# Sliding-window stores: 237 direct stores of 32 rows become 60 row scatters of 128 rows

## The chip, the cores and the metric

One core of one Trainium2 chip. The metric is the device time of one execution in microseconds (us), median of several runs. The profile is one further execution; its span is some 2 us shorter than the run time. All runs quoted are fast: granted clock 1.0. A kernel is compared with runs of the kernel before on the same chip.

## The reference

```python
batch, c, h, w = (16, 64, 64, 64); window_size = 8; stride = 4      # float32
n_h = n_w = 15
result = np.zeros((batch, n_h, n_w, c, 8, 8))
for i in range(n_h):
    for j in range(n_w):
        result[:, i, j] = x[:, :, 4*i : 4*i + 8, 4*j : 4*j + 8]
```

Nothing is computed. 16.78 MB are read, 58.98 MB written (each pixel lies in up to four windows).

## The kernel before

The whole input lies in SBUF as `L`, one partition per (image b, channel half ch, band q of 16 image rows), partition p = 8b + 4ch + q. For each window column j and slot s, DVE packs one window per partition into a tile `g` of 8 KB per partition, 1 MiB in all. Partition (b, ch, q) then holds half a row of the output, window row i = 4q + s. The last slot needs rows from the next band and has no window for q = 3.

```python
    HQ = 4; CH = 2; CL = 32; RB = 16; NSLOT = 4
    L = lpool.tile([P, CL, RB, W], f32)                       # 128 KB per partition
    o_v = out.rearrange("b i j (ch cl) r w -> i j b ch (cl r w)", ch=CH)
    ...                                                       # 16 loads of 1 MiB on ACT
    for j in range(NW):
        for s in range(NSLOT):
            g = gpool.tile([P, CL, WS, WS], f32, name="g")    # 9 buffers
            chunks = NCH if j == 0 and s == 0 else 1          # first tile in four pieces
            ...
                if s < NSLOT - 1:
                    nc.vector.tensor_copy(out=g[:, cs], in_=L[:, cs, s*ST : s*ST + WS, cols])
                else: ...                                     # copy of half a window, shuffle of the other
                for q in range(HQ):
                    i = NSLOT * q + s
                    if i < NH:
                        nc.sync.dma_start(out=o_v[i, j, :, :, ...], in_=g[q::HQ, cs, :, :])
```

One store takes every fourth partition: 32 rows of 8 KB, 256 KB. On the HBM side its shape is 16 images x 2 channel halves x 2048 elements.

Of the kernel before, what the change touches and what calls it, by code (L numbers as in the profile page):

```python
# [1 line left out]

# [4 lines left out]


@with_exitstack  # L10
def kernel(
    ctx: ExitStack,
    tc: tile.TileContext,
    x: bass.AP,
    window_size: int,
    stride: int,
    out: bass.AP,
):
    nc = tc.nc
    P = nc.NUM_PARTITIONS  # L20

    B, C, H, W = x.shape
    Bo, NH, NW, Co, WSo, WSo2 = out.shape
    WS = int(window_size)
    ST = int(stride)
    assert Bo == B and Co == C and WSo == WS and WSo2 == WS

    f32 = mybir.dt.float32

    HQ = 4  # L30
    CH = P // (B * HQ)
    CL = C // CH
    RB = H // HQ
    NSLOT = RB // ST
    assert WS == 2 * ST

    lpool = ctx.enter_context(tc.tile_pool(name="lpool", bufs=1))
    gpool = ctx.enter_context(tc.tile_pool(name="gpool", bufs=9))


    L = lpool.tile([P, CL, RB, W], f32)
    x_v = x.rearrange("b (ch cl) (hq r) w -> hq (b ch) cl (r w)", ch=CH, hq=HQ)
    o_v = out.rearrange("b i j (ch cl) r w -> i j b ch (cl r w)", ch=CH)
    NCH = 4
    cw = CL // NCH
    for k in range(NCH):
        for q in range(HQ):
            nc.scalar.dma_start(  # L48
                out=L[q::HQ, k * cw : (k + 1) * cw, :, :],
                in_=x_v[q, :, k * cw : (k + 1) * cw, :],  # L50
            )

    nxt = [min(p + 1, 31) for p in range(32)]
    CFREE = CL * WS * WS
    for j in range(NW):
        cols = slice(j * ST, j * ST + WS)
        for s in range(NSLOT):
            g = gpool.tile([P, CL, WS, WS], f32, name="g")
            chunks = NCH if j == 0 and s == 0 else 1
            n = CL // chunks  # L60
            for k in range(chunks):
                cs = slice(k * n, (k + 1) * n)
                if s < NSLOT - 1:
                    nc.vector.tensor_copy(out=g[:, cs, :, :], in_=L[:, cs, s * ST : s * ST + WS, cols])  # L64
                else:

                    nc.vector.tensor_copy(out=g[:, cs, 0:ST, :], in_=L[:, cs, s * ST : RB, cols])  # L67
                    nc.vector.stream_shuffle(out=g[:, cs, ST:WS, :], in_=L[:, cs, 0:ST, cols], mask=nxt)  # L68
                for q in range(HQ):
                    i = NSLOT * q + s  # L70
                    if i < NH:
                        nc.sync.dma_start(  # L72
                            out=o_v[i, j, :, :, k * CFREE // chunks : (k + 1) * CFREE // chunks],
                            in_=g[q::HQ, cs, :, :],
                        )


# [1 line left out]
_INS = ['x', 'window_size', 'stride']  # L79
_OUTS = [((16, 15, 15, 64, 8, 8), 'float32')]  # L80

_NUMBERS = {'window_size': 8, 'stride': 4}


# [26 lines left out]
```

## Time and profile before

| | value |
|---|---|
| time | 222.07 us (221.17 to 224.38, 3 runs) |
| loads | to 45.8 us, 409 GB/s |
| stores | 50 to 220 us, 339 to 345 GB/s, DMA share 0.95 to 0.97 |
| 8 KB store packet | median 309 ns, mean 365 ns |
| DVE busy | 82.9 us, 37% |

Packet times are from the trace's record of each DMA packet: when it started on its DMA engine and how long it took. The page and the windows are read in the prediction.

### The profile page before, as it was taken

Reading aid. Unit: us, or ns where it says so; the run is one execution under the profiler, and the core shown is the slowest. Engines: PE = TensorE matmul, PEld = TensorE weight load, DVE = VectorE, ACT = ScalarE, POOL = GpSimd, SP = SyncE. Lnnn points to the kernel's source line nnn. Section 1 sums busy time; section 2 is a strip of 40 time slices with the busy share of each in tenths; the row PEclk is TensorE's granted clock in tenths of the full one; section 3 lists DMA queues with packets and bytes.
Section 4 is the critical chain, followed back from the end, with each engine's and each line's share of the span. In section 5 each row is a group of like instructions: output and inputs, shape, how many; then the busy total and the mean of one; then the engine's idle time right before and its main releaser. Section 6 shows DMA issues by size and latency. Waiting matters only on the chain.

```text
span 222.1 us, 564 instructions
## 1 busy us (share of the span) xinstructions
DVE 82.9 (37%) x93; POOL 0.2 (0%) x4
## 2 busy tenths in 40 slices
DVE  0000000069946354454526453535454545430000
POOL 0000000000000000000000000000000000000000
DMA  5999999928999999999999999999999999999995
GB/s 210 418 409 412 412 413 409 412 103 285 337 356 351 328 350 344 334 344 337 341 339 348 359 341 342 353 347 335 360 353 342 332 354 334 329 347 335 326 359 215
DMA packets 15733, 75.81 MB, mean 341 GB/s; under 512 B 4049, under 2 KB 4049, under 8 KB 8657
## 3 DMA queue, kind: packets, MB, share of 16 engines
q1 hardware_dynamic: 11376, 59.00, 74.9%
q10 hardware_dynamic: 4352, 16.78, 18.9%
q14 instruction: 5, 0.03, 0.0%
HBM read 16.78 MB, written 58.98 MB: 341 GB/s over the span
## 4 chain that ended last, share of the span: by engine, by line
SPq 59%; DMA 22%; issue 5%; DVE 2%; ACTq 1%; DVEq 0%
SPq L72 59%; DMA L<-in_x_dram 20%; DMA out_dram<-g 3%; ACTq L48 1%; DVE g L64 1%; DVE g L68 1%; DVE g L67 0%; DVEq L64 0%; DVEq L67 0%
## 5 line engine op out<-in xcount | busy, mean ns | idle before, releaser
L64 DVE COPY g<-L 128x2048 f32<-128x2048 f32 (+1 forms) x48 | 55.1, 1159 | 93.2 <-DMA out_dram<-g 47.9
L68 DVE STREAM_SHUFFLE g<-L 128x1024 f32<-128x1024 f32 x15 | 19.2, 1278 | 0.0
L67 DVE COPY g<-L 128x1024 f32<-128x1024 f32 x15 | 10.4, 693 | 21.9 <-DMA out_dram<-g 21.9
L68 DVE LOAD_MASK_SELECT g<-L x15 | 0.2, 15 | 0.0
L92 POOL MEMSET const-bfloat16-1.0<- 128x1 bf16 x1 | 0.1, 102 | 0.0
L92 POOL MEMSET const-uint8-127<- 128x1 uint8 x1 | 0.1, 102 | 0.0
L92 POOL MEMSET const-float32-0.0<- 128x1 f32 x1 | 0.1, 99 | 0.2 <-issue 0.2
L92 POOL MEMSET const-float32-1.0<- 128x1 f32 x1 | 0.1, 99 | 0.0
## 6 DMA issues: line engine op xcount, KB each, us to landing
out_dram<-g SPq DMA_DIRECT2D x221, 256.0 KB, 3.8
L<-in_x_dram ACTq DMA_DIRECT2D x16, 1024.0 KB, 10.8
out_dram<-g SPq DMA_DIRECT2D x16, 64.0 KB, 5.1
```

What stands on the lines that cost most here:

```text
L48: nc.scalar.dma_start(out=L[q::HQ, k * cw : (k + 1) * cw, :, :], in_=x_v[q, :, k * cw : (k + 1) * cw, :],)
L64: nc.vector.tensor_copy(out=g[:, cs, :, :], in_=L[:, cs, s * ST : s * ST + WS, cols])
L67: nc.vector.tensor_copy(out=g[:, cs, 0:ST, :], in_=L[:, cs, s * ST : RB, cols])
L68: nc.vector.stream_shuffle(out=g[:, cs, ST:WS, :], in_=L[:, cs, 0:ST, cols], mask=nxt)
L72: nc.sync.dma_start(out=o_v[i, j, :, :, k * CFREE // chunks : (k + 1) * CFREE // chunks], in_=g[q::HQ, cs, :, :],)
L92: nc = _bacc.Bacc("TRN2", target_bir_lowering=False, num_devices=1)
```

## The change

The intent: one scatter per tile instead of four direct stores. Each partition has an index, computed once: the output row (of 8 KB) that it fills. A scatter takes all 128 partitions; the tile's j and s are an offset added to the index. Where a row is to be skipped (q = 3 in the last slot), a second index is past the end and the row is dropped. The scatters are issued from gpsimd (POOL), so the stores leave SP; loads are dealt to SP and ACT; the first tile is no longer cut in four.

```diff
-            nc.scalar.dma_start(                                  # loads
+            (nc.sync, nc.scalar)[q % 2].dma_start(
...
+    nc.gpsimd.iota(pi[:, :], pattern=[[0, 1]], base=0, channel_multiplier=1)
+    ...                     # nine DVE instructions on 128x1: idx = b*450 + q*120 + ch
+    ...                     # idx_last = idx, plus 14400 where q == 3
+    o_v = out.rearrange("b i j (ch cl) r w -> (b i j ch) (cl r w)", ch=CH)
...
-                for q in range(HQ):
-                    i = NSLOT * q + s
-                    if i < NH:
-                        nc.sync.dma_start(out=o_v[i, j, ...], in_=g[q::HQ, cs, :, :])
+            st = nc.gpsimd.indirect_dma_start(
+                out=o_v,
+                out_offset=bass.IndirectOffsetOnAxis(ap=(idx_last if last else idx)[:, 0:1], axis=0),
+                in_=g.rearrange("p c r w -> p (c r w)"), in_offset=None,
+                element_offset=(s * NW + j) * CH * CFREE,
+                bounds_check=B * NWIN * CH - 1, oob_is_err=False)
+            tc.declare_no_dep(st.ins, group="stores", reason="each store writes rows of its own")
```

More of the change, by code (lines that the diff above doesn't have):

```diff
@@ L28 @@
     f32 = mybir.dt.float32
+    i32 = mybir.dt.int32
+    ALU = mybir.AluOpType
     HQ = 4
@@ L34 @@
     NSLOT = RB // ST
-    assert WS == 2 * ST
+    NWIN = NH * NW
+    CFREE = CL * WS * WS
+    assert HQ == 4 and CH == 2 and WS == 2 * ST
     lpool = ctx.enter_context(tc.tile_pool(name="lpool", bufs=1))
+    ipool = ctx.enter_context(tc.tile_pool(name="ipool", bufs=1))
     gpool = ctx.enter_context(tc.tile_pool(name="gpool", bufs=9))
@@ L42 @@
     x_v = x.rearrange("b (ch cl) (hq r) w -> hq (b ch) cl (r w)", ch=CH, hq=HQ)
-    o_v = out.rearrange("b i j (ch cl) r w -> i j b ch (cl r w)", ch=CH)
     NCH = 4
@@ L51, with itile @@
             )
+    def itile(name):
+        return ipool.tile([P, 1], i32, name=name)
+    pi, tb, tq, tc_, idx, idx_last = (itile(n) for n in ("pi", "tb", "tq", "tc", "idx", "idx_last"))
+    nc.gpsimd.iota(pi[:, :], pattern=[[0, 1]], base=0, channel_multiplier=1)
+    nc.vector.tensor_scalar(out=tb[:, :], in0=pi[:, :], scalar1=3, scalar2=None, op0=ALU.logical_shift_right)
+    nc.vector.tensor_scalar(out=tc_[:, :], in0=pi[:, :], scalar1=2, scalar2=1, op0=ALU.logical_shift_right, op1=ALU.bitwise_and)
+    nc.vector.tensor_scalar(out=tq[:, :], in0=pi[:, :], scalar1=HQ - 1, scalar2=None, op0=ALU.bitwise_and)
+    nc.vector.tensor_scalar(out=tb[:, :], in0=tb[:, :], scalar1=float(NWIN * CH), scalar2=None, op0=ALU.mult)
+    nc.vector.tensor_tensor(out=tb[:, :], in0=tb[:, :], in1=tc_[:, :], op=ALU.add)
+    nc.vector.tensor_scalar(out=tc_[:, :], in0=tq[:, :], scalar1=float(NSLOT * NW * CH), scalar2=None, op0=ALU.mult)
+    nc.vector.tensor_tensor(out=idx[:, :], in0=tb[:, :], in1=tc_[:, :], op=ALU.add)
+    nc.vector.tensor_scalar(out=tq[:, :], in0=tq[:, :], scalar1=float(HQ - 1), scalar2=float(2 * B * NWIN * CH), op0=ALU.is_equal, op1=ALU.mult)
+    nc.vector.tensor_tensor(out=idx_last[:, :], in0=idx[:, :], in1=tq[:, :], op=ALU.add)
+    o_v = out.rearrange("b i j (ch cl) r w -> (b i j ch) (cl r w)", ch=CH)
     nxt = [min(p + 1, 31) for p in range(32)]
-    CFREE = CL * WS * WS
     for j in range(NW):
@@ L58 @@
             g = gpool.tile([P, CL, WS, WS], f32, name="g")
-            chunks = NCH if j == 0 and s == 0 else 1
-            n = CL // chunks
-            for k in range(chunks):
-                cs = slice(k * n, (k + 1) * n)
-                if s < NSLOT - 1:
-                    nc.vector.tensor_copy(out=g[:, cs, :, :], in_=L[:, cs, s * ST : s * ST + WS, cols])
-                else:
-                    nc.vector.tensor_copy(out=g[:, cs, 0:ST, :], in_=L[:, cs, s * ST : RB, cols])
-                    nc.vector.stream_shuffle(out=g[:, cs, ST:WS, :], in_=L[:, cs, 0:ST, cols], mask=nxt)
-                for q in range(HQ):
-                    i = NSLOT * q + s
-                    if i < NH:
-                        nc.sync.dma_start(
-                            out=o_v[i, j, :, :, k * CFREE // chunks : (k + 1) * CFREE // chunks],
-                            in_=g[q::HQ, cs, :, :],
-                        )
+            last = s == NSLOT - 1
+            if not last:
+                nc.vector.tensor_copy(out=g[:, :, :, :], in_=L[:, :, s * ST : s * ST + WS, cols])
+            else:
+                nc.vector.tensor_copy(out=g[:, :, 0:ST, :], in_=L[:, :, s * ST : RB, cols])
+                nc.vector.stream_shuffle(out=g[:, :, ST:WS, :], in_=L[:, :, 0:ST, cols], mask=nxt)
+            st = nc.gpsimd.indirect_dma_start(
+                out=o_v,
+                out_offset=bass.IndirectOffsetOnAxis(ap=(idx_last if last else idx)[:, 0:1], axis=0),
+                in_=g.rearrange("p c r w -> p (c r w)"),
+                in_offset=None,
+                element_offset=(s * NW + j) * CH * CFREE,
+                bounds_check=B * NWIN * CH - 1,
+                oob_is_err=False,
+            )
+            tc.declare_no_dep(st.ins, group="stores", reason="each store writes rows of its own")
+            tc.add_to_no_dep_group("stores", st.ins)
 _INS = ['x', 'window_size', 'stride']
```

## The prediction

> **What bounds the kernel now.** The kernel is pure data movement: 16.78 MB of images are loaded, the vector engine (DVE) packs windows into tiles g of 1 MiB, 58.98 MB of windows are stored. I read the busy strip first, to find the stages.
>
> ```profile
> ## 2 busy tenths in 40 slices
> DVE  0000000069946354454526453535454545430000
> ...
> DMA  5999999928999999999999999999999999999995
> GB/s 210 418 409 412 412 413 409 412 103 285 337 356 351 328 350 344 334 344 337 341 339 348 359 341 342 353 347 335 360 353 342 332 354 334 329 347 335 326 359 215
> ```
>
> Each slice is 5.55 us. Three stages: loads at about 410 GB/s up to 45 us, a hole near 46 to 51 us (slice 9, 103 GB/s), then stores at about 343 GB/s. So the stores run 16% slower than the loads on the same 16 DMA engines, although those are called busy throughout. A table by stage confirms it; its columns are window, length, DVE busy, POOL busy, clock, DMA share, GB/s:
>
> ```profile
> 14.00:45.50 31.50, 1.19 (x3) 0.00 (x0) 1.00 1.02 409
> 45.50:51.00 5.50, 4.58 (x7) 0.00 (x0) 1.00 0.29 73
> 51.00:100.00 49.00, 29.31 (x32) 0.00 (x0) 1.00 0.96 339
> 100.00:150.00 50.00, 23.85 (x26) 0.00 (x0) 1.00 0.96 345
> ...
> 200.00:220.00 20.00, 0.00 (x0) 0.00 (x0) 1.00 0.95 339
> ```
>
> From 200 us on DVE has nothing left to do and the rate is still 339 GB/s: neither DVE nor the nine g buffers set it. It is either the transfers or the sync engine (SP) that issues them. The chain that ended last names SP:
>
> ```profile
> SPq 59%; DMA 22%; issue 5%; DVE 2%; ACTq 1%; DVEq 0%
> ```
>
> The timeline and the view of the store's line show how SP issues:
>
> ```profile
> 99.71 25.75 SPq L72 DMA_DIRECT2D out_dram<-g  x34
> ```
>
> ```profile
> L72 SPq DMA_DIRECT2D out_dram<-g x237: 536/644/1385, 14.4 to 217.3; - x119
> ...
> DMA to landing us min/median/max: 1.9/3.8/5.2
> ```
>
> SP issues without a break, 34 stores in 25.75 us, 0.757 us each; a tile needs four of them (one per row group q), 3.03 us. The next line has the shortest, median and longest issue in ns: 0.54 us where nothing holds it up, 0.64 usually. A 256 KB store is two 8 KB packets on each of 16 DMA engines. The packet records of the trace give an 8 KB packet at 309 ns for 60% of them (2 x 309 = 0.62 us), but 364 ns on average. So an issue takes about as long as the transfer that it starts, and each can make the other wait. Where I follow one DMA engine from packet to packet, about a quarter of the stores start after a small hole, and their first packet is then often over 500 ns; at the very first store after the hole all 16 first packets took 539 to 700 ns and the 16 after them 309. Loads, with 16 packets per engine and issue, have 159 ns (median) per 4 KB packet and 164 on average. My reading: **the stores lose their 16% because they are fed in small pieces, just in time**. 309 ns per packet would be 16 x 8192 B / 309 ns = 424 GB/s.
>
> [...]
>
> **The change part by part.**
> - *Removed*: 237 store issues on SP. *Added*: 60 scatters on POOL, one per tile, of 128 rows of 8 KB (96 rows in the 15 tiles with s = 3, where the rows q = 3 lie past the end and are skipped). The rows stay 45 x 128 + 15 x 96 = 7200, the bytes the same 58.98 MB in the same 8 KB packets. Per DMA engine that is 450 packets if the rows spread evenly, 8 per scatter, with one completion instead of four per tile.
> - *Loads* now from two queues, SP and ACT. The loads already run at 409 to 418 GB/s with issues of 0.61 us for 1 MiB (one landing each 2.7 us): worth about 0.
> - *Index arithmetic*: one iota and nine DVE instructions on 128x1, long over before the first load chunk lands (DVE first works at 13.9 us). Worth 0.
> - *The first tile is no longer cut in four*: 3 x 256 KB that were stored under the loads move behind them. The DMA engines were full in both places: loads end 0.79 MB / 410 GB/s = 1.9 us earlier, and the bytes are paid later. But the hole grows: before, a 0.43 us copy and a 0.54 us issue came ahead of the first late store; now a full 1.23 us copy and the first descriptor generation.
> - *Order*: the scatters are declared independent; each waits only for its copy and, from the ninth on, for the scatter eight earlier. Some eight scatters of about 2.5 us can be queued, so POOL's delay is hidden as long as its throughput is enough.
>
> The sum. Last load lands 46.2 - 1.9 = 44.3 us, DVE starts 44.5, copy done 45.7. First scatter's descriptors and first packet: 2 us, an estimate (the shortest issue to landing before was 1.9 us; nothing shows a scatter). Stores begin at 47.7. Rate: packets of 309 ns with what remains of disturbance. In runs of packets that follow each other without a hole I found about 330 and 347 ns for the first and second of a store; fewer completions should help, so I take 330 ns (an estimate): 450 x 0.330 = 148.5 us, 397 GB/s. Tail from the last packet to the end, as before: 219.9 to 222.1, 2.2 us. Together 47.7 + 148.5 + 2.2 = 198.4; I say **199 us**, 10% faster.
>
> **The rivals.**
> 1. *POOL becomes the bound.* A tile on the DMA engines is 148.5 / 60 = 2.5 us. DVE's copies per tile are (45 x 1.226 + 15 x 0.693) / 60 = 1.09 us[...]. If generation takes G and the two exclude each other wholly, POOL needs 1.09 + G. Up to G = 1.4 us nothing is lost; G = 1.8 gives 2.9 per tile, 174 us, 224 in all, no gain; G = 2.3 gives 253.[...] Against it: the author's choice of this form, and the eight scatters of slack, which smooth but do not add throughput.
> 2. *HBM writes are the limit, not the feeding.* Then 343 GB/s stays: 172 us of stores, 222 in all, same. For it: even unbroken runs show a third of second packets over 330 ns. Against it: 60% of packets at exactly 309 ns[...].
> 3. *Full gain*: every packet at 309 ns, 139 us, 189 in all.
> 4. *Uneven engines*: skipped rows falling on the same DMA engines[...]. If a few engines get all 8 rows in every scatter they carry 480 packets instead of 450: 10 us more, 209.
>
> **Range and chances.** Central 199. Rivals 3 and 4 span 189 to 209; rival 1 has the long tail upward, rival 2 sits at 222. I give POOL as bound about 0.25 (half of it beyond 226 us), HBM as limit about 0.12. Low 187, high 228; faster 0.70, same 0.13, slower 0.17.
>
> **What would show it.** Right: stores at 385 to 420 GB/s in the strip, DMA share 1.0, mean 8 KB packet 320 to 340 ns, DVE waiting for landed stores, POOL's issues waiting for scatters to complete. POOL as bound: DMA share well under 0.9 in the store stage, scatters issued back to back, the chain on POOL's queue, and gaps that line up with DVE copies. HBM as limit: share 1.0, 343 GB/s, packets still 364 ns on average. Start wrong: first store later than 48 us. The prediction is wrong if G, which no trace here shows, exceeds about 1.5 us[...].

Passages that say of the hardware what no trace or run of this case shows are cut out of the recorded texts, here and in the expectations; the cuts are marked. "The two exclude each other wholly" in rival 1 was an assumption; e4 measures what there is of it. "Descriptors" and "generation" (G) name the time that POOL is busy with one scatter, 0.96 to 2.43 us in the changed kernel; what POOL does in that time no trace shows.

## The result, and the profile after

201.17 us (200.99 to 201.24, 4 runs) against 222.22 us: faster, ratio 0.904 (95% interval 0.8973 to 0.9108). A ratio is the mean time of one kernel's fast runs over that of the other's fast runs of the same rounds, so it is not quite the ratio of the medians.

The busy strip of the changed kernel, in 40 slices of 4.98 us:

```profile
DVE  2000000009996646464657474746464646430000
POOL 0000000006888787545455555555555555540000
DMA  5999999972999999999999999999999999999961
GB/s 189 419 405 410 410 414 410 409 303 92 401 398 410 406 405 400 408 405 413 405 411 415 408 405 411 411 406 405 413 406 408 406 413 406 406 411 414 419 286 43
```

After the hole the stores now run at the rate of the loads; only the last two slices fall off. The same by stage (window, length, DVE busy, POOL busy, clock, DMA share, GB/s):

```profile
14.00:43.00 29.00, 0.00 (x0) 0.00 (x0) 1.00 1.03 410
...
100.00:150.00 50.00, 28.57 (x31) 26.98 (x21) 1.00 1.01 408
...
180.00:190.00 10.00, 0.00 (x0) 0.00 (x0) 1.00 1.01 415
190.00:194.00 4.00, 0.00 (x0) 0.00 (x0) 1.00 0.64 268
194.00:196.00 2.00, 0.00 (x0) 0.00 (x0) 1.00 0.34 139
```

The store rate went from 343 to 408 GB/s at a DMA share of 1.01 instead of 0.96. Loads are as fast as before, two queues or one. The packet records give the same picture: the mean 8 KB packet fell from 365 to 322 ns. At the end half of the DMA engines have their last packet at about 191.2 us and the other half at about 195.4 us, so the last 4 us run at half rate or less. POOL, new in this kernel, is seen best in the groups (count, busy us, mean ns, idle before and its cause):

```profile
L86 POOL DMA_INDIRECT out_dram<-g,idx x45 | 60.5, 1344 | 86.4 <-DVE g L82 45.2
...
L86 POOL DMA_INDIRECT out_dram<-g,idx_last x15 | 19.6, 1308 | 11.4 <-DVE g L85 9.6
```

In the timeline around the start, two scatters show what stretches them:

```profile
44.62 3.50 DVE L82 COPY g<-L 128x2048 f32<-128x2048 f32 x3 [42.46 <-DMA L<-in_x_dram]
46.14 2.10 POOL L86 DMA_INDIRECT out_dram<-g,idx  x1 [45.19 <-DVE g L82]
...
53.84 1.26 DVE L85 STREAM_SHUFFLE g<-L 128x1024 f32<-128x1024 f32 x1
54.45 0.96 POOL L86 DMA_INDIRECT out_dram<-g,idx  x1 [0.30 <-issue]
```

Beside a run of copies the first scatter took 2.10 us; beside a shuffle one took 0.96 us. The median is 1.38. Even so, POOL is busy only half of the store stage, and it is 4% of the chain that ended last ("issue" is time for which the profile shows no wait):

```profile
DMA 51%; issue 34%; POOL 4%; POOLq 1%; PEldq 0%
```

A scatter's issue to landing is 18.7 us: some eight are queued.

One more thing is in the packet counts. The scatters' queue has 8640 packets: 7200 rows, 60 x 16 = 960 completions, and 480 more of 4 bytes, exactly the 15 x 32 skipped rows. I infer that a skipped row still costs a tiny packet; the 4-byte packets take 7 to 9 ns each, so it costs almost nothing here. (The page's HBM line counts 62.91 MB written, 3.93 MB too many, which is 480 rows of 8 KB: it seems to count skipped rows in full. The queue moved 58.99 MB.)

### The profile page after: what moved, and what is told of

Same layout as the page of the kernel before. It is cut to its first block, busy times and chain, and to the rows that moved or that the text cites. A ratio compares the mean times of both kernels' runs of the same rounds, so it can differ in the third digit from the quotient of the medians.

```text
span 199.2 us, 395 instructions
## 1 busy us (share of the span) xinstructions
DVE 83.8 (42%) x99; POOL 80.4 (40%) x65
## 3 DMA queue, kind: packets, MB, share of 16 engines
q0 software_dynamic: 8640, 58.99, 73.2%
HBM read 16.78 MB, written 62.91 MB: 400 GB/s over the span
## 4 chain that ended last, share of the span: by engine, by line
DMA 51%; issue 34%; POOL 4%; POOLq 1%; PEldq 0%
DMA out_dram<-g,idx_last 51%; POOL out_dram L86 4%; POOLq L127 1%; POOLq L86 0%; POOL pi L62 0%; PEldq L127 0%
## 5 line engine op out<-in xcount | busy, mean ns | idle before, releaser
L86 POOL DMA_INDIRECT out_dram<-g,idx x45 | 60.5, 1344 | 86.4 <-DVE g L82 45.2
L82 DVE COPY g<-L 128x2048 f32<-128x2048 f32 x45 | 55.1, 1235 | 75.3 <-DMA L<-in_x_dram 42.5
L86 POOL DMA_INDIRECT out_dram<-g,idx_last x15 | 19.6, 1308 | 11.4 <-DVE g L85 9.6
## 6 DMA issues: line engine op xcount, KB each, us to landing
out_dram<-g,idx POOLq DMA_INDIRECT x45, 18.7
```

Source lines behind the costliest of these rows:

```text
L82: nc.vector.tensor_copy(out=g[:, :, :, :], in_=L[:, :, s * ST : s * ST + WS, cols])
L86: st = nc.gpsimd.indirect_dma_start(out=o_v, out_offset=bass.IndirectOffsetOnAxis(ap=(idx_last if last else idx)[:, 0:1], axis=0), in_=g.r ...
```

## The experiments

The time agreed with the prediction at once. The question was whether its reason did: that 256 KB stores, issued just in time by one queue, starved the DMA engines.

| run | time, us | ratio to before | store stage, GB/s | mean packet, ns | over 330 ns |
|---|---|---|---|---|---|
| before | 222 to 224 | 1 | 339 to 345 | 362 | 36% |
| changed kernel | 201.17 | 0.904 | 406 to 409 | 323 | 17% |
| e1_two_queues | 218.75 | 0.985 | 346 to 354 | 366 | 32% |
| e4_copies_on_act | 201.94 | 0.908 | 406 to 409 | 323 | 16% |
| e6_chunked_start | 200.61 | 0.902 | 401 to 409 | 323 | 17% |
| e9_half_scatters | 237.51 | 1.068 | 306 to 315 | (4 KB packets) | |
| e5_wide_direct (wrong rows) | 194.78 | 0.875 | 415 to 421 | 314 | 11% |
| e10_four_buffers (wrong rows) | 194.71 | 0.871 | 416 to 420 | 314 | 11% |
| e7_deep_direct (wrong rows) | 195.80 | 0.880 | 409 to 420 | 315 | 3% |
| e11_two_rows (wrong rows) | 196.05 | 0.877 | 406 to 417 | 315 | 10% |
| e12_one_row (wrong rows) | 199.15 | 0.891 | 399 to 409 | 315 | 0.2% |
| e14_one_row_by_image (wrong rows) | 226.05 | 1.010 | 327 to 352 | 364 | 36% |
| e13_direct_and_scatter | 291.34 | 1.300 | 251 to 325 | 385 | 35% |
| e15_start_filled | 203.32 | 0.909 | 408 to 409 | 323 | 16% |

Store rates are from windows between 50 and 180 us (e15 from 100 on); packet figures are 8 KB packets that start between 60 and 180 us, from the trace's records. "Wrong rows" means that the kernel writes all output bytes, but to other rows than it should.

### e1: the kernel before with two issuing queues

```diff
-                        nc.sync.dma_start(
+                        (nc.sync, nc.scalar)[q % 2].dma_start(
```

> The kernel before with its 256 KB stores issued in turn by SP and ACT, everything else as before: same packets, same rows per DMA engine, same two-packet stores with one completion each. Theory A (one queue's issue cadence of 0.757 us feeds the DMA engines just in time): the cadence per store can halve, so the store stage rises from 343 to 395 GB/s or more, mean 8 KB packet under 335 ns, time 198 to 206 us. Theory B (a completion after every two packets, or which partitions' rows a DMA engine reads, costs the time): nothing of that changes, 343 GB/s within 8, packet mean about 364 ns, time 219 to 225 us.

218.75 us, ratio 0.985 (0.9776 to 0.9918). The store stage hardly moved. The windows of e1, and the view of its store line (min/median/max of one issue in ns):

```profile
51.00:100.00 49.00, 28.45 (x32) 0.00 (x0) 1.00 0.99 352
100.00:150.00 50.00, 23.51 (x25) 0.00 (x0) 1.00 0.98 346
```

```profile
L72 SPq DMA_DIRECT2D out_dram<-g x126: 535/1122/1851, 14.5 to 211.9; - x126
L72 ACTq DMA_DIRECT2D out_dram<-g x111: 542/1204/1894, 32.6 to 201.0; - x111
```

With two queues each issue takes nearly twice as long (median 1122 and 1204 ns against 644), so I read the issues as waiting for the DMA engines and not the engines for issues. The holes closed (share 0.96 to 0.99), which is worth the 1.5%, but the packets are as long as before. Theory A falls as the main cause; the time is just under the 219 to 225 us of theory B.

### e5: wide direct stores in place of scatters

A correct direct store of a whole tile would need image x half x band x elements on the HBM side; the builder refused it ("Unable to balance aps with more than 3 dims"). So e5 takes rows that step evenly, which are the wrong ones:

```diff
-            st = nc.gpsimd.indirect_dma_start(...)
+            # o_v: out as b (i j ch) (cl r w);  NT = 56
+            nc.sync.dma_start(out=o_v[:, t : 8 * NT : NT, :], in_=g.rearrange("p c r w -> p (c r w)"))
```

> The changed kernel with each scatter replaced by one direct store of 128 rows (1 MB) on SP's queue: no POOL, no index. The rows go to wrong places on purpose[...], so the result is wrong; packets, bytes and rows per DMA engine (8 per store, one completion) are as in the scatter. If the gain comes from the wide store (theory C: one completion per 8 packets instead of per 2, or theory P: which partitions an engine reads), the store stage is at 400 to 415 GB/s, 196 to 202 us. If it comes from the scatter's software descriptors or queue (theory S): about 345 GB/s, 218 us or more.

194.78 us, a little better than expected:

```profile
100.00:150.00 50.00, 27.82 (x31) 0.00 (x0) 1.00 1.01 420
```

The gain is not a property of scatters; direct wide stores are 3% faster still. Theory S is out, and with it the idea that HBM writes are the limit.

### e7, e11, e12: stores of 8, 4 and 2 packets per DMA engine, same partitions as before

e7 packs the four slots of one j into one tile of 32 KB per partition and stores, for each q, 32 partitions x 4 rows. e11 and e12 split that into two rows and one row per store. e12 thus has 225 stores of 256 KB on SP alone, like the kernel before. In the queue's packet count each store comes with 16 completions: beside the 7200 rows e7 has 960 packets more (60 stores), e11 1920 (120), e12 3600 (225); the kernel before has 3792 for 237 stores. "Per DMA engine" takes the rows as evenly spread over the 16.

```diff
+        gv = g.rearrange("p s c r w -> p s (c r w)")
-                        nc.sync.dma_start(out=o_v[i, j, ...], in_=g[q::HQ, cs, :, :])
+                # o_v: out as 32 x 225 x (cl r w); rows lo, lo+60, ... ; n = 4 (e7), 2 (e11), 1 (e12)
+                nc.sync.dma_start(out=o_v[:, lo + 60*r : ... : 60, :], in_=gv[q::HQ, r : r + k, :])
```

> The kernel before with four tiles gathered into one of 32 KB per partition and each store taking 32 partitions (every fourth, as before) times four rows of 8 KB: 1 MB per store, 8 packets per DMA engine and completion[...]. Rows go to wrong places on purpose. The start is later by some 4 us (four copies ahead of the first store) and not chunked, so read the store stage. Theory C (completions after every two packets cost the time): 395 to 415 GB/s there, packet mean under 335 ns, 200 to 208 us. Theory P (which partitions an engine reads): 345 GB/s within 10, packet mean about 360 ns, 222 us or more.

> As e7_deep_direct, but each store takes two rows of the four-row tile instead of four: 4 packets per DMA engine and completion, twice the stores, the same partitions and row spacing (wrong rows on purpose). Theory C (each completion costs a DMA engine a fixed time, 2 x (364 - 309) = 110 ns as before and 44 ns in e7): packet mean 320 to 337 ns, 390 to 410 GB/s in the store stage, 198 to 206 us. If the gain of e7 came from rows of one partition that follow each other without regard to completions: 418 GB/s as e7, 196 us.

> As e7_deep_direct with one row per store: 256 KB, 2 packets per DMA engine and completion, as in the kernel before, but with the tile layout and row spacing of e7. Theory C: back to 340 to 355 GB/s, packet mean about 360 ns, 218 to 227 us. If e7 gained by its layout or row spacing: stays above 395 GB/s, under 206 us.

e7 came out at 195.80 us, which fitted theory C (a cost per completion). Theory P as e7 stated it fell: the same 32 partitions per store gave 409 to 420 GB/s instead of 345. (e14 takes up P again, for the HBM side's shape.) e11, at 196.05, fitted it poorly: its packets were no longer than e7's. e12 broke it: 199.15 us, 409 GB/s, mean packet 315 ns, with two packets per completion, 256 KB per store and one queue. Its store line, the chain by engine and a window:

```profile
L70 SPq DMA_DIRECT2D out_dram<-g x225: 468/596/602, 50.0 to 193.8; - x113
```

```profile
SPq 58%; DMA 15%; ACTq 9%; issue 5%; DVE 5%; DVEq 1%
```

```profile
100.00:150.00 50.00, 28.20 (x32) 0.00 (x0) 1.00 1.00 409
```

The chain says SP 58%, as it did before (59%), while the rate is 409 instead of 345. So that line of the chain did not tell what held the stores back in the kernel before. Small pieces, one queue and many completions are all present in e12, and none of them costs what the kernel before lost. What they do cost is the difference of e12 to e7, 3.3 us across two chips, or to e11 on the same chip, 3.1 us.

### e10: fewer bytes in flight

e5 with `bufs=4` for g instead of 9.

> As e5_wide_direct with four g buffers instead of nine, so that at most three stores of 1 MB are in flight instead of eight. Rival theory F (what counts is bytes in flight: 8 stores of 256 KB before, 8 of 1 MB after): the rate falls well under 400 GB/s, 205 us or more. Theory C: packets per completion are unchanged, packet mean stays under 325 ns, 195 to 199 us.

194.71 us, as e5. With stores of this shape, four buffers serve as well as nine; the shape of the kernel before was not tried with another number.

### e14: e12 with the store's HBM side split by image

What was left between e12 and the kernel before was the shape of one store. On the SBUF side both take 32 partitions in steps of four. On the HBM side e12 has 32 even steps, the kernel before 16 images x 2 halves. e14 changes that and almost nothing else:

```diff
-    o_v: out as m n (cl r w), m = 32, n = 225;            out=o_v[:, row, :]
+    o_w: out as b c n (cl r w), b = 16, c = 2, n = 224;   out=o_w[:, :, row, :]
```

> As e12_one_row, with the same bytes, packets, issues and completions, and row addresses almost the same (the two channel halves 224 rows apart instead of 225, again wrong rows on purpose), but the store's two sides no longer split alike: its HBM side is 16 images x 2 halves (as in the kernel before), not 32 even steps. Theory P[...]: back to 335 to 355 GB/s, packet mean about 360 ns, first 16 packets over 530 ns, 218 to 228 us. Theory H (the kernel before was slow because each engine wrote two neighbouring rows, 16 KB in one place of HBM, at a fixed distance): the rows are still far apart, so 399 to 415 GB/s and 199 to 202 us as e12.

226.05 us against e12's 199.15 from the same packets, issues and completions: the time that theory P named. What P supposed of the engines' reading no trace shows. The store line and the windows of e14:

```profile
L72 SPq DMA_DIRECT2D out_dram<-g x225: 536/679/1413, 50.2 to 221.3; - x113
```

```profile
50.00:100.00 50.00, 21.75 (x26) 0.00 (x0) 1.00 0.93 327
100.00:150.00 50.00, 24.79 (x30) 0.00 (x0) 1.00 0.96 338
```

Everything that marked the kernel before is back: DMA share 0.96, mean packet 364 ns with 36% over 330, issues of up to 1.4 us. The very first packets are telling, because the first 16 start together after the hole (within 0.27 us in the trace before):

| run | HBM side of a store | first 16 packets, ns | next packets, ns |
|---|---|---|---|
| before | 16 x 2 | 539 to 700 | 309 |
| e14 | 16 x 2 | 546 to 702 | 309 |
| e5 | 16 x 8 | 339 to 640 | about 600, then falling to 312 |
| e12 | 32 | 315 to 324 | 309 to 315 |
| changed kernel | scatter of 128 | 309 to 318 | 307 to 312 |

So the slow first packets before were no start-up cost. In these runs they appear only where the HBM side starts with the 16 images. They do not last equally long: in e5 the mean of 32 packets in a row falls from 679 to 314 ns within some 300 packets; before and in e14 the packets that follow the slow first 16 take 309 ns, and yet the mean over the stage stays at 362 to 364. Why packets of this shape take longer was not shown.

What is shown: the shape of one store, with row addresses nearly unchanged, moves the rate from 409 to 338 GB/s. What is not shown is how: the packet records name neither the DMA engine nor the partitions that it reads. A rival remains: the two halves of an image lie 224 x 8 KB = 1792 KB apart in e14 and 1800 KB in e12, and no run varied that distance alone. The set of addresses by itself is not the cause, since the correct scatter writes the very rows of the kernel before, at 408 GB/s; the order in which the engines write them may be.

### e4: no copy beside the scatters

```diff
-                nc.vector.tensor_copy(out=g[...], in_=L[...])
+                nc.scalar.copy(out=g[...], in_=L[...])
```

> The changed kernel with its tile copies on ACT instead of DVE (the shuffles stay on DVE)[...]. If the lock is what lengthens scatters, nearly all take the 0.96 us of the shortest ones (median now 1.38, longest 2.43). Theory A (POOL has slack in the store stage): the rate stays 405 to 410 GB/s and the time 199 to 203 us, the same within 1%. Rival (the packets over 309 ns and the slower half of the DMA engines come from that contention): rate 414 or more, time 197 us or less.

"The lock", here and in e9, stands for DVE's copies holding up a scatter: supposed when this was written, measured below.

201.94 us. The view of the scatter line (min/median/max in ns):

```profile
L86 POOL DMA_INDIRECT out_dram<-g,idx x45: 957/962/1114, 48.0 to 176.6; - x45
```

Now nearly every scatter takes 0.96 us, so DVE's copies are what stretched them to 1.38. How, the changed kernel's timeline shows:

```profile
101.86 1.23 DVE L82 COPY g<-L 128x2048 f32<-128x2048 f32 x1 [1.21 <-DMA out_dram<-g,idx]
102.54 1.39 POOL L86 DMA_INDIRECT out_dram<-g,idx  x1 [1.05 <-DMA out_dram<-g,idx]
```

The scatter starts in the middle of a copy, the copy ends 0.55 us later, and the scatter ends 0.84 us after that. Other scatters that start inside a single copy, with 0.18 to 0.93 us of it left, end 0.82 to 0.84 us after the copy too: they make almost no progress until it is over (some 0.12 of its 0.96 us in the scatter above). The rate did not move: in the changed kernel that stretch is hidden. ACT needs 1.90 us for a copy that takes DVE 1.23, which delays the first scatter from 46.1 to 48.0 us; as that scatter is then shorter, the first packet comes at 49.7 us instead of 48.8, about the 0.8 us by which e4 is slower than the changed kernel. The packets of 316 ns and more are not due to the copies either.

### e9: how far POOL is from being the bound

Each scatter cut into two of 4 KB rows: the index doubled, two scatters per tile.

> The changed kernel with each scatter cut into two, of 128 rows of 4 KB: twice the scatters, same bytes. If generation costs by scatter and row, each takes 0.96 us alone and is followed by 0.3 us: 2 x 1.26 = 2.5 us per tile, plus about half a copy of lock, 3.0 us per tile against 2.4 that the DMA engines need: POOL is the bound, 234 us (266 if copies and scatters exclude each other wholly). If generation costs by bytes, or is hidden anyway: 201 us within 2%.

237.51 us. The windows of e9, and its scatter line:

```profile
100.00:150.00 50.00, 24.57 (x25) 40.25 (x33) 1.00 0.78 315
```

```profile
L89 POOL DMA_INDIRECT out_dram<-g,idx x90: 959/968/2427, 46.2 to 227.3; - x90
```

A scatter of half the bytes takes the same 0.96 us: the cost does not go by bytes. (Each still has 128 rows, so a cost per scatter and one per row are not told apart.) 33 scatters start in 50 us, 1.5 us each, so a tile costs POOL 3.0 us, the estimate written beforehand. DMA share falls to 0.78. In the changed kernel a tile takes the DMA engines 2.4 us and POOL 1.34 + 0.3 = 1.6 us; twice the scatters would tip it over.

### e6, e15: the start

e6 stores the first tile as the kernel before does (four pieces, directly, under the loads) and puts all loads back on ACT. e15 does the same with a second tile, in halves.

```diff
+            if j == 0 and s == 0:
+                for k in range(NCH): ...   # copy a quarter, four direct stores on SP
+                continue
```

> The changed kernel with the first tile stored as before (four copies and 16 stores of 64 KB by SP under the loads) and all loads on ACT as before; the other 59 tiles are scatters. 1 MB leaves the store stage (2.5 us at 408 GB/s), three quarters of it go under the loads, which end 1.9 us later. The hole stays. Expected 199 to 202 us, within 1% of the changed kernel: if the two-queue loads had helped, it would be slower by what they brought; if the start's order mattered more than bytes, 197 or less.

> A correct version meant to beat both: e6_chunked_start with the second tile also stored directly by SP (two halves, eight stores of 128 KB), to fill the hole while POOL generates its first scatters; 58 tiles by scatter. First store after the loads about 1.5 us earlier than in the changed kernel (48.2 us), 1 MB of direct stores[...]: 198.5 to 201 us. If the first scatters come later because POOL waits for DVE's run of copies, no better than e6 (200.6 us).

e6: 200.61 us (200.49 to 200.68), 0.6 us under the changed kernel's runs. Its ratio to the kernel before, 0.902, is not told apart from 0.904 by their intervals. e15: 203.32 us, over the 198.5 to 201 expected. Its loads slowed to 185 and 354 GB/s between 25 and 35 us and its last load chunk was copied at 51.0 us instead of 46.5; why was not followed up.

### e13: a correct version with direct stores for most tiles

Partitions reordered to p = 64ch + 4b + q, so that the bands and images of one half make an even block; two direct stores of 512 KB (16 x 4 x 2048) per tile, scatters for the last slot.

> A correct version meant to beat both: partitions reordered so that the channel half is outermost; tiles without skipped rows (45 of 60) are stored by two direct stores of 512 KB on SP and ACT (4 packets per DMA engine and completion), the 15 tiles with skipped rows by a scatter as in the changed kernel. From e5 and e7 (415 to 420 GB/s direct, 8 packets) and one more completion per tile: about 410 GB/s in the store stage, first store 1 us earlier than the changed kernel's: 195 to 200 us. If 64 partitions per store cost bandwidth: 205 us or more.

291.34 us, a miss by far. The windows of e13:

```profile
14.00:43.00 29.00, 0.00 (x0) 0.00 (x0) 1.00 1.03 237
...
150.00:180.00 30.00, 10.56 (x12) 4.17 (x2) 1.00 0.77 251
```

Even the loads, now of 16 partitions each, fell from 410 to 237 GB/s at full DMA share (mean 4 KB load packet 284 ns instead of 164), and most of the first 64 store packets took about 592 ns. A load or store now stays in one half of the partitions, and the load's steps through HBM changed as well; the run does not tell the two apart, and why the packets take longer was not shown.

## Why the prediction was right or wrong

**The time: right.** 199 us stated, 201.17 measured (span 199.2).

**The sum, term by term.** DVE started its copies at 44.62 us (predicted 44.5). The first packet came at 48.8 us (47.7), past the 48 us that the prediction named as the sign of a wrong start: the first scatter took 2.10 us beside DVE's run of copies, and the sum had left that out of this term. Stores took 146.8 us from the first packet to the last (148.5), on average at 402 GB/s (397) and 322 ns per packet (330). The tail was 3.6 us (2.2; in the profile before, the last packet ended at 220.7 us and not at 219.9, so the tail there was 1.4). The errors of +1.1, -1.7 and +1.4 us largely cancel, which is luck. Loads on two queues and index arithmetic were worth nothing, as stated.

**The reading of the bound: wrong.** The step that failed is "the stores lose their 16% because they are fed in small pieces, just in time". e1 took away the single queue: 218.75 us. e12 kept the small pieces, one queue and the completions, and ran at 409 GB/s. e14 changed little but the shape of one store on its HBM side, and fell to 338. The kernel before lost its time through the 16 x 2 shape of its stores (packets of 364 ns on average in e14 against 315 in e12); how that shape makes them longer was not shown. The scatter has 128 rows in one list, and its first packets show none of it (309 to 318 ns). As e5 and e12 show, the gain needs no scatter and no larger or fewer stores. That the start-up packets of 539 to 700 ns were read as a refill after a hole was the same error: e12, after the same kind of hole, has 315 to 324. The number came out because both readings promise the same, packets near 309 ns: as regards the mechanism, that is luck.

**The rivals.** POOL as bound: not here, but the estimate behind it (1.09 us of copies per tile and an unknown generation time G) was of the right kind: G is 0.96 us alone, 1.34 on average, and e9 shows the bound at twice the scatters. The two do not exclude each other in full: e9's tile took 3.0 us, not 2 x 1.26 + 1.09 = 3.6 (its scatters were stretched by some 0.28 us each, from 0.96 to 1.24 on average). HBM writes as limit: out, at 408 to 421 GB/s. Full gain: the direct wide stores came nearest, 194.7. Uneven engines: half of the engines finish 4.2 us early. Each scatter ends in one completion per engine; eight of the 16 lag, by some 0.2 us at 66 us and by 4.0 us at 184 us, so the lag builds up over the whole stage. If the rows are shared evenly (the records don't say), that is an uneven pace, not uneven work. Its cause stays open, as does the difference of the scatters' 408 GB/s to e5's 420; e4 rules out the copies for both.

## What to carry to other kernels

When DMA engines are called busy but move less than the same engines do elsewhere in the trace, compare the packets' times before blaming the issuing queue, and test the queue by adding a second one. Then try the same transfer in another shape: here an HBM side in even steps, as the SBUF side has them, ran at 409 GB/s and one of 16 x 2 at 338, with little else changed. Where the right rows don't fit a direct store's dimensions, a row scatter is a way to get there, as long as POOL's time per scatter (1.6 us here, with the 0.3 us gap) stays under the transfer's (2.4 us).
